# Retention pairs with both heads' scores in one matmul, queries decayed in turned form, a folded Fourier branch and nine steps a pair

## The chip, the cores and the metric

The kernel runs on one core of a Trainium2 chip. The metric is the device time of one execution in microseconds (us); the median of three runs of the kernel before is 1471.9. Engines are named as in the profile: PE (TensorE matmuls), DVE (VectorE), ACT (ScalarE), POOL (GpSimd), SP (the engine that issues most DMAs).

## The reference

Two transformer blocks over 512 positions of width 1024 in float32. The first (forgetting attention, a short convolution, a mixture of 16 experts, a per-layer embedding) is not touched by the change. The second has a bidirectional chunked retention, a Fourier mix, a gated merge of the two and a convolutional feed-forward part. The two branches that change, cut:

```
def chunk_retention(q, k, v, a, s0):        # 8 heads, dk 64, dv 128, CHUNK = 128
    diff = pos[:, None] - pos[None, :]
    intra_decay = where(diff >= 0, exp(lg * max(diff, 0)), 0)
    scores = einsum('bhncd,bhnsd->bhncs', qc, kc) * intra_decay
    intra = einsum('bhncs,bhnse->bhnce', scores, vc)
    k_dec = kc * exp(lg * (CHUNK - 1 - pos))
    kv = einsum('bhnsd,bhnse->nbhde', k_dec, vc)
    s_final, s_prev = scan(s -> exp(lg * CHUNK) * s + kv_n, s0, kv)
    q_dec = qc * exp(lg * (pos + 1))
    inter = einsum('bhncd,nbhde->bhnce', q_dec, s_prev)
    return intra + inter, s_final

o = chunk_retention(forward) + flip(chunk_retention(flipped))
o = (o - mean) * rsqrt(var + EPS)           # over dv, then * silu(g), then @ w_ret_out

def fourier_mix(f, w_f):                    # 4 groups of 128
    z = fft2(f.reshape(b, 512, 4, 128), axes=(1, 3), norm='ortho').real
    return z @ w_f
```

## The kernel before, in words

Every float32 matmul is made of three products of high and low parts: `split` (L186) writes the high part with a copy on ACT and the low part with a subtraction on DVE, `mm3` (L202) issues the three matmuls. Weights come by DMA into one of three `raw` slots (`new_raw`), are split into `whi` and `wlo` (`wsplit`), and a `Feed` (L117) keeps three weight splits ahead of the matmuls that use them. Tiles of 1024 columns come from a pool of 5 (`T`), of 512 columns from a pool of 35 (`B`); the accumulators come from four `pmm`, two `psd` and two `ptr` banks. A scheduler sets the order of each engine's instructions from the order of the program and its own estimate of readiness, so what stands side by side in a queue need not stand side by side in the code.

The retention works on pairs of heads, g = 0 to 3. `ret_proj(g)` projects q, k, v and the gate of pair g; q and k land as rows of positions in `qkr`. `ret_core` (L1504) turns q and k of a pair on PE (`pt_qk`, 8 transposes a pair), splits them, and loads the pair's decay factors `dmt` from a table `dmat` in HBM that `decays` (L637) has made early on. `ret_head` (L1547) is one head as a sequence of steps: queries and keys are decayed as rows of positions (tq and tk, L1553), the decayed queries are turned on PE (`pt_qd`, L1560) and split; scores of the head are 12 matmuls with 64 rows contracted (`ps_sc`), multiplied by the decay factors (`sc`, L1570) and split; `ps_kv` is 12 matmuls; the state recurrences (st, L1585 and L1588) work on the lower 64 partitions forward and the upper 64 backward; `ps_o` is 16 matmuls (L1604 to L1607). Then come `on` and its statistics on DVE, the reciprocal root on POOL (rs_e, rs_r), `nmr` on DVE, the normalisation `on` on ACT (L1626), the transposes `pt_o` (L1630) and the product with the gate (sg, L1631). `ret_cores` (L1528) deals the steps of a pair's two heads out in eight steps; a head's last steps are left for the next pair (`late`).

`fourier` (L1638) projects f in four groups of feature rows (`project`, `ps_f`, split into fT), multiplies along dims by a 128x256 table of cosines and sines (`along_dims`, two groups at a time: 24 matmuls of 256 columns, then half, fold and a split), and along rows by a table of 512x512 that is split in two pieces of 1024 columns (`along_rows`, 24 matmuls a group), into zT.

The driver sets the order: pair 0's projection runs alone, pairs 1 to 3 are projected while the steps of the pair before run beside them (a step of the retention for three of the projection), and the Fourier branch runs beside the last pair with ratio R_FOUR. Behind both come ret_out (`ps_ro`), which needs the split outputs `oT` of all pairs, the Fourier output, the branch gates and the merge.

```
    run(proj[0])
    cores = ret_cores()
    for g in range(1, 4):
        interleave(proj[g], islice(cores, 8), 1 / 3)
    interleave(four, cores, R_FOUR)
```

Of the kernel before, what the change touches and what calls it, by code (L numbers as in the profile page):

```python
# [21 lines left out]
P = 128  # L22
S = 512
# [14 lines left out]
R_FOUR = 0.37  # L38
# [9 lines left out]
def constants():  # L48
# [25 lines left out]
    once = np.concatenate([causal, tri, dec, dft1], 1)  # L74
    n = np.arange(S // 2)
    k = np.concatenate([2 * n, 2 * n + 1])
    w512 = 2 * np.pi * (np.outer(n, k) % S) / S
    dft2 = np.concatenate([np.cos(w512), -np.sin(w512)], 0) / 256.0
# [16 lines left out]
def weave(main, side, ratio, drain=True, acc=0.0):  # L95

    for _ in main:
        acc += ratio
        while side is not None and acc >= 1.0:
            acc -= 1.0  # L100
            next(side, 0)
        yield 1
    if side is not None and drain:
        yield from side
# [35 lines left out]
def fused_blocks(ctx, tc, a, out, probe=None, upto=99):  # L140
# [494 lines left out]
    dmat = drm.tile([P, D], F32, name="dmat")  # L635

    def decays():  # L637
# [21 lines left out]
        sp.dma_start(dmat, dm[0])  # L659
# [844 lines left out]
    def ret_core(g):  # L1504
# [5 lines left out]


        qkT = []
        for i in range(2):
# [3 lines left out]
            h, l = B("qk2_hi", F32R), B("qk2_lo", F32R)  # L1517
            if i == 0:
                act.activation(h, pt, AF.Copy, scale=0.125)
                dve.scalar_tensor_tensor(l, pt, 0.125, h.bitcast(F32), op0=ALU.mult, op1=ALU.subtract)  # L1520
            else:
                split(pt, h, l)
            qkT.append((h, l))
        dmt = B("dmt", w=256)
        sp.dma_start(dmt, dmat[:, 2 * c:2 * c + 256])
        return [ret_head(2 * g + hh, hh, rv, qkT, v, sg, dmt[:, hh * P:(hh + 1) * P]) for hh in range(2)]

    def ret_cores():  # L1528
# [3 lines left out]
        for g in range(4):  # L1532
            one_, two = ret_core(g)
# [13 lines left out]
    def ret_head(hd, hh, rv, qkT, v, sg, dmh):  # L1547

        tq, tk = B("tq"), B("tk")
        for tt, i in ((tq, 0), (tk, 1)):  # L1550
            tv = v3(tt, NT)
            for b in range(2):
                dve.tensor_scalar(tv[:, :, 64 * b:64 * b + 64], rv(i, hh), dec[:, 4 * b + i, hd:hd + 1], None,  # L1553
                                  op0=ALU.mult)
# [6 lines left out]
        qd = B("qd_hi", F32R), B("qd_lo", F32R)  # L1561
        split(pt, *qd)
        yield 1
        r = slice(64 * hh, 64 * hh + 64)
        ps = psd("ps_sc")
        for n in range(NT):
            cc = slice(n * P, n * P + P)
            mm3(ps[:, cc], [u[r, cc] for u in qkT[1]], [u[r, cc] for u in qkT[0]], True, True)
        sc = B("sc")
        dve.tensor_tensor(v3(sc, NT), v3(ps, NT), bc(dmh[:, None, :], [P, NT, P]), op=ALU.mult)  # L1570
        pT = B("sc_hi", F32R), B("sc_lo", F32R)
        split(sc, *pT)
# [25 lines left out]
        ps = [psd("ps_o") for _ in range(2)]  # L1598
        for n in range(NT):
# [3 lines left out]
            vn = v[n].rearrange("p (s h c) -> p h s c", s=2, h=2)[:, hh]  # L1603
            pe.matmul(hl, qd[0][:, cc], sn, start=True, stop=False)  # L1604
            pe.matmul(v3(hl, 2), pT[0][:, cc], vn, start=False, stop=False)
            pe.matmul(h, qd[1][:, cc], sn[:, :P], start=False, stop=False)
            pe.matmul(h, pT[1][:, cc], vn[:, 0], start=False, stop=True)  # L1607
# [30 lines left out]
    def fourier():  # L1638
# [3 lines left out]
        def load(i):  # L1642
            if i == 0:
                raw.append(new_raw())
                sp.dma_start(v3(raw[0], 4), a["k_dft2"].rearrange("(k p) c -> p k c", p=P))
            return wsplit(raw[0][:, i * 1024:(i + 1) * 1024], 1024)

        dft_nos = feed.plan([lambda i=i: load(i) for i in range(2)])

        def steps():  # L1650
            fT, aT, w = [], {}, []

            def project():
                f = len(fT)
                ps = yield from feat_step(nos[f // 2], h4, "ps_f2")
                h, l = B("fT_hi", F32R), B("fT_lo", F32R)
                split(ps, h, l)
                fT.append((h, l))

            def along_dims(gp):  # L1660

                for t in range(2):
                    ps = [pmm("ps_d1") for _ in range(2)]
                    for u in range(2):
                        for i in range(2):
                            x = [y[:, (t + 2 * u) * P:(t + 2 * u + 1) * P] for y in fT[2 * gp + i]]
                            mm3(ps[u][:, i * 256:i * 256 + 256], x, dft1, True, True)
# [194 lines left out]
```

## Time and profile before

| | |
|---|---|
| median of 3 runs | 1471.9 us (1471.68 to 1473.94) |
| the profiled execution | 1473.61 us |
| its span | 1471.5 us |
| mean granted PE clock | 0.994 |
| busy: PE, DVE, ACT, POOL | 1426.3, 989.4, 737.8, 115.5 us |

A span is the time from the first to the last instruction of the core. In the profile's rows a matmul's own duration overlaps that of the next one, so that the price of one in a row of many is the distance of two starts. The retention with the Fourier branch takes from about 700 to 888 us of the span: pairs begin (`pt_qk`) at 700.64, 745.46, 790.67 and 835.73, and ret_out begins at 888.52.

### The profile page before, as it was taken

The page shows a single profiled execution, that of the slowest core. Times are in us where ns is not written, and L with a number is a line of the kernel's source. Part 1 is how long each engine was busy: PE and PEld are TensorE (multiplying, and loading weights), DVE is VectorE, ACT ScalarE, POOL GpSimd, SP SyncE. Part 2 cuts the span into 40 slices and gives each one's busy share as a digit, 9 for nine tenths or more (in the row PEclk, how much of TensorE's full clock was granted, in tenths as well). Part 3 has the DMA queues.
Part 4 walks back from the last instruction along what each step waited for, and adds up shares of the span by engine and source line. Part 5 has one row for each costly group of instructions (what it writes and reads, how often), then busy time and mean ns, then how long its engine had stood idle before and what let it go on. Part 6 is the DMA issues. An engine that isn't in the chain of part 4 may idle for free.

```text
span 1471.5 us, 18307 instructions
## 1 busy us (share of the span) xinstructions
PE 1426.3 (97%) x6885; PEld 1156.6 (79%) x6885; DVE 989.4 (67%) x1590; ACT 737.8 (50%) x1201; POOL 115.5 (8%) x136
## 2 busy tenths in 40 slices
PE   6999999999999999799999999999999999999997
PEld 5777788887877676677888888888778888888886
DVE  6677764796899996655776777466665653465644
ACT  5765653434479887665444454334264442244422
POOL 1410000000031311200000000000000000000001
PEclk9999999999999999999999999999999999999999
DMA  6231234556679998323222115656623323343311
GB/s 227 71 123 59 81 121 156 174 202 257 195 253 375 394 389 309 131 67 105 89 63 90 62 58 170 202 175 212 201 57 93 108 79 97 97 115 86 104 54 57
DMA packets 150886, 219.15 MB, mean 149 GB/s; under 512 B 9728, under 2 KB 101388, under 8 KB 150796
## 3 DMA queue, kind: packets, MB, share of 16 engines
q1 hardware_dynamic: 145548, 201.05, 41.2%
q0 software_dynamic: 3456, 10.62, 2.2%
q10 hardware_dynamic: 1792, 6.29, 1.1%
q8 instruction: 55, 0.90, 0.2%
q14 instruction: 35, 0.29, 0.1%
HBM read 206.76 MB, written 11.17 MB: 148 GB/s over the span
## 4 chain that ended last, share of the span: by engine, by line
PE 53%; ACT 3%; DVE 2%; POOL 1%; issue 1%; POOLq 0%; ACTq 0%
PE ps_tok L206 6%; PE ps_tok L205 6%; PE ps_tok L204 6%; PE ps_up L204 6%; PE ps_up L205 6%; PE ps_up L206 6%; PE ps_gt L205 2%; PE ps_gt L206 2%; PE ps_gt L204 2%; PE ps_g L204 1%; PE ps_g L206 1%; PE ps_g L205 1%; PE ps_ro L204 1%; PE ps_ro L206 1%; PE ps_ro L205 1%
## 5 line engine op out<-in xcount | busy, mean ns | idle before, releaser
L188 DVE TENSOR_TENSOR wlo<-raw,whi 128x1024 fp32r<-128x1024 f32 x248 | 300.2, 1215 | 248.3 <-ACT whi L187 241.1
L187 ACT CAST whi<-raw 128x1024 fp32r<-128x1024 f32 x248 | 258.2, 1044 | 297.0 <-PE ps_tok L206 116.9
L204 PE MATMUL ps_up<-nt_hi,whi 128*128 128x512 f32 (+2 forms) x368 | 141.4, 385 | 2.8 <-ACT nt_hi L187 2.8
L205 PE MATMUL ps_up<-nt_lo,whi 128*128 128x512 f32 (+2 forms) x368 | 141.4, 384 | 0.0
L206 PE MATMUL ps_up<-nt_hi,wlo 128*128 128x512 f32 (+2 forms) x368 | 141.2, 384 | 0.0
L204 PE MATMUL ps_tok<-whi,nt_hi 128*128 128x512 f32 x288 | 115.2, 402 | 2.2 <-ACT nt_hi L187 2.1
L206 PE MATMUL ps_tok<-whi,nt_lo 128*128 128x512 f32 x288 | 113.1, 395 | 0.7 <-DVE nt_lo L188 0.7
L205 PE MATMUL ps_tok<-wlo,nt_hi 128*128 128x512 f32 x288 | 113.2, 395 | 0.0
L205 PE MATMUL ps_gt<-nt_lo,whi 128*128 128x512 f32 x256 | 99.6, 389 | 0.0
L204 PE MATMUL ps_gt<-nt_hi,whi 128*128 128x512 f32 x256 | 99.6, 389 | 0.0
L206 PE MATMUL ps_gt<-nt_hi,wlo 128*128 128x512 f32 x256 | 99.6, 389 | 0.0
L719 DVE SCALAR_TENSOR_TENSOR mod_acc<-raw,silu_c,mod_acc 128x1024 f32<-128x1024 f32 x56 | 70.7, 1279 | 20.2 <-DMA raw<-in_w_mod_dram 19.8
L204 PEld LDWEIGHTS ps_up<-nt_hi,whi 128*128 128x128 f32 x368 | 69.7, 190 | 16.0 <-ACT nt_hi L187 3.0
L205 PEld LDWEIGHTS ps_up<-nt_lo,whi 128*128 128x128 f32 x368 | 69.7, 189 | 13.3 <-DVE nt_lo L188 0.2
L206 PEld LDWEIGHTS ps_up<-nt_hi,wlo 128*128 128x128 f32 x368 | 69.7, 189 | 13.2
L188 DVE TENSOR_TENSOR wlo<-raw_a,whi 128x1024 fp32r<-128x1024 f32 x56 | 68.1, 1241 | 1.5 <-ACT whi L187 1.5
L204 PE MATMUL ps_tok<-whi,hid_hi 128*128 128x512 f32 x176 | 68.5, 389 | 0.0
L205 PE MATMUL ps_tok<-wlo,hid_hi 128*128 128x512 f32 x176 | 68.5, 389 | 0.0
L206 PE MATMUL ps_tok<-whi,hid_lo 128*128 128x512 f32 x176 | 68.3, 389 | 0.0
L204 PEld LDWEIGHTS ps_tok<-whi,nt_hi 128*128 128x128 f32 x288 | 54.7, 190 | 14.7 <-ACT nt_hi L187 3.6
L206 PEld LDWEIGHTS ps_tok<-whi,nt_lo 128*128 128x128 f32 x288 | 54.7, 190 | 13.0 <-DVE nt_lo L188 1.9
L187 ACT CAST whi<-raw_a 128x1024 fp32r<-128x1024 f32 x56 | 57.8, 1052 | 11.6 <-PE ps_tok L206 7.0
(461 smaller groups left out, 3291.8 us busy)
## 6 DMA issues: line engine op xcount, KB each, us to landing
raw<-in_w_in_dram SPq DMA_DIRECT2D x31, 1024.0 KB
raw<-in_w_up_dram SPq DMA_DIRECT2D x55, 512.0 KB
raw<-in_w_mod_dram SPq DMA_DIRECT2D x24, 1024.0 KB
raw<-in_w_down_dram SPq DMA_DIRECT2D x15, 1024.0 KB
raw_a<-in_w_gate_dram SPq DMA_DIRECT2D x19, 512.0 KB
raw_a<-in_w_up_dram SPq DMA_DIRECT2D x19, 512.0 KB
raw_a<-in_w_down_dram SPq DMA_DIRECT2D x9, 1024.0 KB
raw<-in_w_branch_gate_dram SPq DMA_DIRECT2D x8, 1024.0 KB
```

Source lines behind the costliest of these rows:

```text
L187: act.copy(hi, src)
L188: return (eng or dve).tensor_tensor(lo, src, hi.bitcast(F32), op=ALU.subtract)
L204: pe.matmul(ps, x[0], y[0], start=first, stop=False)
L205: pe.matmul(ps, x[0], y[1], start=False, stop=False)
L206: pe.matmul(ps, x[1], y[0], start=False, stop=last)
L719: dve.scalar_tensor_tensor(ac, rv[:, j, :], col, ac, op0=ALU.mult, op1=ALU.add)
```

## The change

- `decays`: beside the table for the scores a second one holds, for each head and both directions, the factors of the decayed queries in turned form (16 Exps of 64x128 on ACT, one more DMA of 512 KB); two small scalings on DVE go.
- `ret_core` is now a sequence of steps. The turned queries of both heads are split into tiles that hold the two heads in blocks of a diagonal, with zeros beside them (four memsets of 64x4x128 a pair on POOL), so that one matmul over 128 rows and 256 columns gives the scores of both heads: 12 matmuls a pair instead of 24. The decayed queries come from the turned ones in PSUM times the new factors (four instructions of 64x512 a pair on DVE); the transposes `pt_qd` go. `dmt` is 256 KB a pair, of 128 before, and is asked for ahead of `pt_qk`.
- `fourier` folds f along the feature axis before the matmuls along dims, so that each group needs 12 matmuls of 128 columns and 3 of one output row; the table along rows is folded too, 128x1024, one DMA of 512 KB and one split, and takes 12 matmuls a group. Its split stands at the start of the branch's code. Dims and rows of the groups alternate with the projections.
- A pair has nine steps, steps can weigh less than one, and R_FOUR is 0.5.

```diff
 def weave(main, side, ratio, drain=True, acc=0.0):
-    for _ in main:
-        acc += ratio
+    for step in main:
+        acc += ratio * step
...
+        for h in range(8):
+            r = slice(64 * (h % 2), 64 * (h % 2) + 64)
+            for b in range(2):
+                o = h // 2 * 256 + b * P
+                act.activation(dq[r, o:o + P], C("iota")[r, :], AF.Exp, ...)
+        sp.dma_start(dmat[:, 1], dq)
...
-        dmt = B("dmt", w=256)
-        sp.dma_start(dmt, dmat[:, 2 * c:2 * c + 256])
+        dmt = B("dmt")
+        sp.dma_start(v3(dmt, 2), dmat[:, :, 2 * c:2 * c + 256])
...
+        for u in q4:
+            for hh in range(2):
+                pool.memset(u[64 * hh:64 * hh + 64, :, 1 - hh, :].bitcast(F32), 0.0)
+        for hh, r in enumerate(rows):
+            act.activation(q4[0][r, :, hh, :], pts[0][r], AF.Copy, scale=0.125)
+            dve.scalar_tensor_tensor(q4[1][r, :, hh, :], pts[0][r], 0.125, q4[0][r, :, hh, :].bitcast(F32),
+                                     op0=ALU.mult, op1=ALU.subtract)
+        split(pts[1], *[v3(u, NT) for u in kT])
+        yield [ret_head(2 * g + hh, hh, rv, v, sg, qds, pT) for hh in range(2)]
+        for r in rows:
+            tq = B("tq")
+            for b, o in enumerate(rows):
+                dve.scalar_tensor_tensor(v3(tq, NT)[o], pts[0][r], 0.125,
+                                         bc(dmt[r, None, 256 + b * P:384 + b * P], [64, NT, P]),
+                                         op0=ALU.mult, op1=ALU.mult)
+            qd = B("qd_hi", F32R), B("qd_lo", F32R)
+            split(tq, *qd)
+            qds.append(qd)
+        yield
+        for j in range(2):
+            ps = psd("ps_sc")
+            for n in (2 * j, 2 * j + 1):
+                mm3(ps[:, n % 2 * 256:n % 2 * 256 + 256], [u[:, n * P:n * P + P] for u in kT],
+                    [u[:, n * 256:n * 256 + 256] for u in qb], True, True)
+            sc = B("sc")
+            dve.tensor_tensor(v3(sc, 2), v3(ps, 2), bc(dmt[:, None, :256], [P, 2, 256]), op=ALU.mult)
+            pT.append((B("sc_hi", F32R), B("sc_lo", F32R)))
+            split(sc, *pT[j])
...
-            for step in ((one_, late), (one_, two, late), (one_,), (two,), (one_,), (two, one_), (one_,), (two,)):
+            for step in ((core, late), (core, one_), (two,), (one_,), (two,), (one_,), (two, one_), (one_,)):
...
-        pt = ptr("pt_qd")
-        for t in range(NT):
-            pe.transpose(pt[:, t * P:(t + 1) * P], tq[:, t * P:(t + 1) * P], ident)
...
                 ps = yield from feat_step(nos[f // 2], h4, "ps_f2")
+                x, uv, y = B("f_rows"), B("f_half"), B("f_fold")
+                act.copy(x, ps)
+                for i, op in enumerate((ALU.add, ALU.subtract)):
+                    dve.tensor_tensor(uv[:, 256 * i:256 * i + 256], x[:, :256], x[:, 256:], op=op)
+                for i, op in enumerate((ALU.add, ALU.subtract)):
+                    dve.tensor_tensor(y4[:, 2 * i:2 * i + 2, 1:], uv2[:, :, 1:P], uv2[:, :, 255:P:-1], op=op)
+                act.copy(y4[:, 0::3, 0], uv4[:, 0::2, 0])
+                act.copy(y4[:, 2:0:-1, 0], uv4[:, 1::2, 0])
+                split(y, h, l)
...
-            for part in (project(), project(), project(), along_dims(0), project(), along_dims(1),
-                         along_rows(0), along_rows(1), along_rows(2), along_rows(3)):
+            for part in (project(), project(), along_dims(0), project(), along_dims(1), along_rows(0), project(),
+                         along_dims(2), along_rows(1), along_dims(3), along_rows(2), along_rows(3)):
...
-        interleave(proj[g], islice(cores, 8), 1 / 3)
+        interleave(proj[g], islice(cores, 9), 9 / 24)
```

The first place is ACT, at the end of pair 2 and the start of the last pair. Before (o_half and on are the outputs of one head, qk_hi the splits of the turned q and k):

```order
L1626 ACTIVATE on<-on,nmr,rs_r 128x128 x4
L187 CAST sc_hi<-sc 128x512
L1582 COPY st<-s_6233 64x128
L1583 COPY st<-s_6233 64x128
L187 CAST st_hl<-st 128x2x128 x2
L187 CAST whi<-raw 128x1024
L1446 ACTIVATE sg_8259<-ps_g 128x512
L187 CAST whi<-raw 128x1024
L1612 COPY o_half<-ps_o 128x256 x2
L1446 ACTIVATE sg_8342<-ps_g 128x512
L1626 ACTIVATE on<-on,nmr,rs_r 128x128 x4
L1519 ACTIVATE qk_hi<-pt_qk_8369 128x512
```

Now (qb_hi and k_hi are the splits of the turned q and k):

```order
L1657 ACTIVATE on<-on,nmr,rs_r 128x128 x4
L1643 COPY o_half<-ps_o 128x256 x2
L1657 ACTIVATE on<-on,nmr,rs_r 128x128 x2
L1459 ACTIVATE sg_8312<-ps_g 128x512
L1657 ACTIVATE on<-on,nmr,rs_r 128x128 x2
L191 CAST whi<-raw 128x1024
L1543 ACTIVATE qb_hi<-pt_qk_8345 64x4x128
L191 CAST k_hi<-pt_qk_8350 128x512
L1543 ACTIVATE qb_hi<-pt_qk_8345 64x4x128
```

Before, the second head's o_half stood behind other work and well after the first head's on; now it stands directly behind the first head's on, the on of both heads stand close together, and the splits of the last pair behind both.

On DVE, what stands around the last pair's splits now (qb_lo are the splits of the two heads' queries, sg the product with the gate, wlo a weight's low part):

```order
L1653 SCALAR_TENSOR_TENSOR nmr<-mv,rs_r 128x4
L1662 TENSOR_TENSOR sg_7754<-sg_7754,pt_o 128x512
L192 TENSOR_TENSOR wlo<-raw,whi 128x1024
L1544 SCALAR_TENSOR_TENSOR qb_lo<-pt_qk_8345,qb_hi 64x4x128
L192 TENSOR_TENSOR k_lo<-pt_qk_8350,k_hi 128x512
L1544 SCALAR_TENSOR_TENSOR qb_lo<-pt_qk_8345,qb_hi 64x4x128
L1552 SCALAR_TENSOR_TENSOR tq<-pt_qk_8345,dmt 64x512 x2
L1662 TENSOR_TENSOR sg_7841<-sg_7841,pt_o 128x512
L192 TENSOR_TENSOR wlo<-raw,whi 128x1024
L192 TENSOR_TENSOR qd_lo<-tq,qd_hi 128x512
L1552 SCALAR_TENSOR_TENSOR tq<-pt_qk_8345,dmt 64x512 x2
```

Before, two qk_lo stood directly behind nmr, and qd_lo behind transposes on PE; now sg and a wlo stand ahead of the splits, tq reads dmt, and qd_lo stands behind tq.

The second place is PE, where the first matmuls along dims (ps_d_8498, of fT of group 0) now stand among those of the third Fourier projection (ps_f_8524):

```order
L210 MATMUL ps_f_8419<-nt_hi,wlo 128x512
L208 MATMUL ps_d_8498<-dft_hi,fT_hi 128x128
L209 MATMUL ps_d_8498<-dft_lo,fT_hi 128x128
L208 MATMUL ps_f_8524<-nt_hi,whi 128x512
L209 MATMUL ps_f_8524<-nt_lo,whi 128x512
L210 MATMUL ps_f_8524<-nt_hi,wlo 128x512
L208 MATMUL ps_f_8524<-nt_hi,whi 128x512
L210 MATMUL ps_d_8498<-dft_hi,fT_lo 128x128
```

Before, the first matmuls along dims stood behind three whole projections.

The third place is SP's queue around the last pair's dmt, now:

```order
L1525 DMA dmt<-dmat 128x2x256
L1677 DMA raw<-in_k_dft_dram 128x1024
L280 DMA raw<-in_w_in_dram 128x8x256
L280 DMA raw<-in_w_ret_out_dram 128x8x256 x2
L1525 DMA dmt<-dmat 128x2x256
L723 DMA raw<-in_w_mod_dram 128x2x1024
```

The last dmt stands behind two ret_out weight loads, as before, and takes twice the bytes; the Fourier table, which stood behind the last projections' weights, is now loaded ahead of the last of them.

## Rows read from the trace of the kernel before

**Rows 1.** The page, part 1: busy time, share of the span and instructions of each engine.
```profile
PE 1426.3 (97%) x6885; PEld 1156.6 (79%) x6885; DVE 989.4 (67%) x1590; ACT 737.8 (50%) x1201; POOL 115.5 (8%) x136
```

**Rows 2.** Windows, pairs 0 to 2: busy us (instructions) per engine, PE clock, DMA share, GB/s.
```profile
700.00:745.00 45.00, 45.00 (x246) 38.24 (x245) 32.38 (x88) 18.60 (x36) 2.13 (x4) 1.00 0.28 87
745.00:790.00 45.00, 45.00 (x248) 38.34 (x248) 32.90 (x90) 19.94 (x40) 2.44 (x5) 1.00 0.23 75
790.00:830.00 40.00, 40.00 (x220) 33.91 (x219) 29.32 (x78) 17.91 (x37) 2.23 (x3) 1.00 0.21 67
```

**Rows 3.** Timeline of PE: start us, us, engine, line, operation, out<-in, shape, count.
```profile
831.56 0.45 PE L204 MATMUL ps_f<-nt_hi,whi 128*128 128x512 f32 x1
...
835.73 1.03 PE L1516 MATMUL pt_qk<-misc,qkr 128*128 128x128 f32 x8
...
845.76 0.32 PE L204 MATMUL ps_sc<-qk_hi 64*128 64x128 f32 x1
...
847.24 0.33 PE L204 MATMUL ps_kv<-v,kd_hi 128*128 128x128 f32 x1
...
853.27 0.28 PE L204 MATMUL ps_d<-dft_hi,fT_hi 128*128 128x256 f32 x1
...
854.69 0.28 PE L1604 MATMUL ps_o<-st_hl,qd_hi 128*128 128x256 f32 x1
...
888.52 0.40 PE L204 MATMUL ps_ro<-oT_hi,whi 128*128 128x512 f32 x1
```

**Rows 4.** The chain of waits, 825 to 895: start us, us, what.
```profile
825.38 0.44 PE pt_o L1630 x4
...
835.04 1.05 POOL rs_r L381
...
890.51 0.52 ACT oT_hi L187
```

**Rows 5.** Windows, the last pair's stretch on DVE, columns as in rows 2.
```profile
838.47:884.57 46.10, 42.96 (x284) 37.99 (x282) 37.88 (x86) 23.95 (x49) 3.15 (x4) 1.00 0.14 47
```

**Rows 6.** Timeline of DVE, last pair; in brackets idle before and releaser.
```profile
838.47 0.69 DVE L1520 SCALAR_TENSOR_TENSOR qk_lo<-pt_qk,qk_hi 128x512 fp32r<-128x512 f32 x1 [2.20 <-ACT qk_hi L1519]
...
839.68 0.61 DVE L1553 TENSOR_SCALAR tq<-qkr,dec 128x256 f32<-128x256 f32 x2
840.20 0.61 DVE L1553 TENSOR_SCALAR tk<-qkr,dec 128x256 f32<-128x256 f32 x2
840.73 1.21 DVE L188 TENSOR_TENSOR wlo<-raw,whi 128x1024 fp32r<-128x1024 f32 x1
...
850.25 0.69 DVE L188 TENSOR_TENSOR sc_lo<-sc,sc_hi 128x512 fp32r<-128x512 f32 x1 [0.74 <-ACT sc_hi L187]
850.86 0.33 DVE L1585 SCALAR_TENSOR_TENSOR st<-st,g,ps_kv 64x128 f32<-64x128 f32 x1
851.22 0.35 DVE L1588 SCALAR_TENSOR_TENSOR st<-st,g,ps_kv 64x128 f32<-64x128 f32 x1
...
853.62 0.76 DVE L188 TENSOR_TENSOR st_hl<-st,st_hl 128x256 fp32r<-128x256 f32 x2 [0.53 <-ACT st_hl L187]
```

**Rows 7.** The instructions of L853: count, ns min/median/max, first and last start.
```profile
L853 DVE SCALAR_TENSOR_TENSOR q_hl<-pt_qk,gq,q_hl x8: 743/749/756, 81.8 to 163.4; 64x512 fp32r<-64x512 f32 x8
```

**Rows 8.** Timeline of ACT at the last pair's start.
```profile
836.31 1.65 ACT L1626 ACTIVATE on<-on,nmr,rs_r 128x128 f32<-128x128 f32 x4 [3.67 <-DVE nmr L1622]
```

**Rows 9.** Timeline of ACT, 58 to 80.
```profile
62.45 0.99 ACT L655 ACTIVATE dm_f<-once,eneg 128x128 f32<-128x128 f32 x3
...
78.81 1.05 ACT L187 CAST whi<-raw 128x1024 fp32r<-128x1024 f32 x1 [4.39 <-PE ps_tok L206]
```

**Rows 10.** Groups of POOL by form: count, busy us, mean ns, idle before.
```profile
L779 POOL TENSOR_TENSOR kdc<-kc,dec 128x256 f32<-128x256 f32 x8 | 11.0, 1398 | 0.1
```

**Rows 11.** Timeline of SP's queue, 815 to 840.
```profile
821.21 11.23 SPq L276 DMA_DIRECT2D raw<-in_w_ret_out_dram  x2
```

**Rows 12.** DMA issues, 80 to 180: count, KB each, median us to landing.
```profile
q_hc<-crows POOLq DMA_DIRECT2D x6, 8.0 KB, 2.4
```

More of the change, by code (lines that the diff above doesn't have):

```diff
@@ L1526, in ret_core @@
-        return [ret_head(2 * g + hh, hh, rv, qkT, v, sg, dmt[:, hh * P:(hh + 1) * P]) for hh in range(2)]
+            pts.append(v3(pt, NT))
+        qb = [T("qb_" + u, F32R) for u in ("hi", "lo")]
+        q4 = [u.rearrange("p (n h c) -> p n h c", h=2, c=P) for u in qb]
+        for u in q4:
+            for hh in range(2):
+                pool.memset(u[64 * hh:64 * hh + 64, :, 1 - hh, :].bitcast(F32), 0.0)
+        kT = [B("k2_" + u, F32R) for u in ("hi", "lo")]
+        rows = [slice(64 * hh, 64 * hh + 64) for hh in range(2)]
@@ L1528, in ret_cores @@
+        yield
     def ret_cores():
@@ L1532, in ret_cores @@
         for g in range(4):
-            one_, two = ret_core(g)
-            for step in ((one_, late), (one_, two, late), (one_,), (two,), (one_,), (two, one_), (one_,), (two,)):
+            core = ret_core(g)
+            next(late, 0)
+            one_, two = next(core)
+            yield 1
+            for step in ((core, late), (core, one_), (two,), (one_,), (two,), (one_,), (two, one_), (one_,)):
                 for h in step:
@@ L1545, in ret_cores, with ret_head @@
             yield 1
[L1547 to L1554, printed above, removed]
+    def ret_head(hd, hh, rv, v, sg, qds, pT):
+        tk = B("tk")
+        tv = v3(tk, NT)
+        for b in range(2):
+            dve.tensor_scalar(tv[:, :, 64 * b:64 * b + 64], rv(1, hh), dec[:, 4 * b + 1, hd:hd + 1], None, op0=ALU.mult)
         kd = B("kd_hi", F32R), B("kd_lo", F32R)
@@ L1557, in ret_head @@
         yield 1
-        pt = ptr("pt_qd")
-        for t in range(NT):
-            pe.transpose(pt[:, t * P:(t + 1) * P], tq[:, t * P:(t + 1) * P], ident)
[L1561 to L1572, printed above, removed]
         ps = psd("ps_kv")
@@ L1603, in ret_head @@
             vn = v[n].rearrange("p (s h c) -> p h s c", s=2, h=2)[:, hh]
+            pn = [u[:, (n % 2 * 2 + hh) * P:(n % 2 * 2 + hh + 1) * P] for u in pT[n // 2]]
             pe.matmul(hl, qd[0][:, cc], sn, start=True, stop=False)
[L1605 removed]
+            pe.matmul(v3(hl, 2), pn[0], vn, start=False, stop=False)
             pe.matmul(h, qd[1][:, cc], sn[:, :P], start=False, stop=False)
[L1607 removed]
+            pe.matmul(h, pn[1], vn[:, 0], start=False, stop=True)
         on = B("on")
@@ L1640, in fourier @@
         raw = []
[L1642 to L1648, printed above, removed]
-        def steps():
-            fT, aT, w = [], {}, []
+        def steps():
+            fT, aT = [], []
+            w = [T("dft2_hi", F32R), T("dft2_lo", F32R)]
+            raw = new_raw()[:, :1024]
+            sp.dma_start(raw, a["k_dft2"])
+            split(raw, *w)
             def project():
```

84 lines of the change are left out of this document (37 added, 47 removed).

## The prediction

> **What bounds the kernel now.** I read the page's first part, then a table by stage, then the chain of waits, and then the timelines of PE, DVE, ACT and SP around the places that the chain names. The profiled execution took 1473.6 us, 1471.5 of it the span; the median shown is 1471.9, so a sum made against the profile is lowered by 1.7 to stand on the median. A change under 0.2% (2.9 us) can't be told from none here.
>
> PE is busy 97% of the span [rows 1]. In the stretches in which pairs 0 to 2 run beside the next pair's projection it is busy every microsecond, 45.00 of 45, 45.00 of 45 and 40.00 of 40, while DVE works 32.4, 32.9 and 29.3 [rows 2]. A matmul taken out there is time taken out, as long as DVE and ACT keep up. The last pair, which runs beside the Fourier branch, is another matter. From the first Fourier projection (831.56) to the first ret_out matmul (888.52) are 56.96 us [rows 3]; the chain leaves PE there, runs through POOL's rsqrt and the splits on DVE and ACT, and is on ACT's oT_hi just ahead of ps_ro [rows 4]. From DVE's first split of q (838.47) to its first split behind the last a_lo (884.57) are 46.1 us: DVE is busy 37.9 of them and idle 8.2, PE is busy 43.0 [rows 5]. Both engines are near their limit in that stretch.
>
> **The change on PE.** The spacing of starts is the price of one matmul. Eight turned queries a pair go; four transposes cost 0.44 on the chain [rows 4], so 0.9. The scores of one head, 12 matmuls, took from 845.76 to 847.24, of two heads 2.96; they become 12 matmuls of 256 columns, which took 1.42 along dims (853.27 to 854.69, 0.118 each) [rows 3]: 1.5 less. That is 2.4 us a pair, 9.6 in all. Along rows 96 matmuls of 256 columns become 48: 5.7 less. Along dims 48 of them (5.7) become 48 of 128 columns and 12 with one output row; at no more than 0.118 each that is 7.1, 1.4 more, and if the one-row ones cost nothing it is no more; I take 1.0 more. PE's whole saving is 9.6 + 5.7 - 1.0 = **14.3 us**; 1459.3 on the profile, 1457.6 on the median, is the floor.
>
> **DVE and ACT.** A pair's queries are now decayed in turned form, in four instructions of 64x512 in place of four of 128x256 (two in 0.52, 839.68 to 840.20) [rows 6]. The nearest row to the new ones is L853, the same operation on 64 partitions, 0.749 us [rows 7]. Full-width neighbours overlap: sc_lo lasts 0.69, and its successor starts 0.61 after it. The st instructions, which alternate between the lower and the upper 64 partitions, last 0.33 and start 0.36 apart: none overlaps [rows 6]. So I take 0.75 for each of the six that alternate in a pair (four tq, two qb_lo): tq costs 2.0 more, and two qb_lo and a k_lo in place of two qk_lo 0.9 more. The Trainium skill (VectorE: DVE Perf Modes, "Two Vector instructions with no wait between them") has a rule that speaks against these six: an instruction whose input or output starts in another group of 32 partitions than the last one's is held until all earlier ones are done. The st rows agree with it. If it didn't hold for them, they would cost 0.61 like full-width ones, the last pair would be 0.84 shorter, and the sum 1467.7 instead of 1468.5.
>
> In the Fourier branch 8 folds and 4 of 8 splits of a go (0.6 each): 7.2. In their place come 8 f_half and 8 f_fold of 256 columns; at 0.34, between tq's 0.26 and st_hl's 0.38 (two in 0.76 [rows 6]), that is 5.4: 1.8 less. The order now puts two z_lo (0.6 each) ahead of the last a_lo: 1.2 more. DVE's work in the stretch becomes 37.9 + 2.0 + 0.9 - 1.8 + 1.2 = **40.2 us**: the folding takes work from PE, not from DVE. ACT is busy 24 of the 46 [rows 5]; its new copies count only as links of a chain.
>
> **Pairs 0 to 2.** DVE gets 2.9 us more a pair and has 11 to 13 idle in each [rows 2], so the first two keep the whole 2.4. Pair 2 gets the split of the Fourier constant (1.2, as wlo [rows 6]) and the lag that its predecessors pass on; of its 2.4 I count 0.6. Together 5.4; the ends are 2.4 (one pair gains) and 7.2 (all three).
>
> **The last pair**, from the first Fourier projection on, is start + work + idle + what follows.
> Start: pt_qk came 4.2 after that projection began [rows 3], behind 18 matmuls; now it stands behind 12, at 2.7. DVE's first split came 2.7 behind pt_qk [rows 3, 6], so it starts at 5.5 at best. But on ACT the second head's o_half of pair 2 now stands behind the first head's on, and the first qb_hi behind both heads' on, so that two rounds through POOL follow each other; in one of them on waited 3.7 for nmr and held ACT from 836.31 to 837.96 [rows 8]. Twice the lag, 5.4, makes it 8.1. I take the middle, 6.8 (now 6.9).
> Work: 40.2.
> Idle: 8.2 if chains cover each other as now. The order sets six more dependent pairs of instructions side by side on DVE, each a round trip through ACT of 0.7 (sc_lo waited 0.74 [rows 6]): a qd_lo, a second sc_lo, a kd_lo and three fT_lo. All paid, 12.4. I take 10.3.
> After the last a_lo stand 12 matmuls along rows, 1.4, with 0.2 of hand-over: 1.6.
> 6.8 + 40.2 + 10.3 + 1.6 = 58.9, against 56.96 now: **2.0 longer**, although PE has some 7 us less to do there. PE will wait at the first ps_d for fT_hi, at ps_kv for kd, and for the last two heads' ps_o and pt_o.
>
> **Edits at nothing.** Of the 16 Exps for the queries' factors eight stand before dm_f at about 61 us: 0.3 each (three dm_f in 0.99), 2.5 us, ahead of 4.4 us in which ACT waits for PE at 78.81 [rows 9]; without that cover, 2.5. The other eight fall into the attention, another 2.5 if PE waited for ACT there. The table's second 512 KB is written long before it is read. The 16 memsets run on POOL, busy 8% [rows 1]; no row shows their size, the nearest (kdc, 256 columns, 1.40 [rows 10]) makes 2.8 each an upper end, and nothing the lower. On SP the last dmt waits behind two ret_out loads, whose issue lasted until 832.44 for want of a raw slot [rows 11]. tq reads it some 9 us after the stretch begins, where the scores read it later; a load of 8 KB lands in 2.4 us [rows 12]. If the slot is freed as now it costs nothing, if it is freed by the wlo that stands just ahead of qb_lo, up to 2.5.
>
> **Sum:** 1473.6 - 5.4 + 2.0 = 1470.2, on the median **1468.5 us**; with the ends of pairs and idle its own range is 1465 to 1472.5.
>
> **Rivals.**
> *PE's saving is kept* (0.28). For it: the order splits the first ps_d group among f2's matmuls, as if fT were there in time, and DVE has 6 us more idle room than work added. With the early start and today's idle the stretch is 5.5 + 40.2 + 8.2 + 1.6 = 55.5, 1.5 shorter, and all pairs give 7.2: 1473.6 - 8.7 - 1.7 = 1463.2. Against it: the six round trips. It holds if they are hidden.
> *The last pair grows by more than the pairs gave: slower* (0.21). The place is DVE's queue between on of pair 2 and tq of pair 3: a late start (8.1), dmt 2.5 late with all behind tq queued, and all round trips paid: 8.1 + 2.5 + 40.2 + 12.4 + 1.6 = 64.8, 7.8 longer. If pairs give 4.8, 1473.6 + 3.0 - 1.7 = 1474.9; if one pair gains, 1477.3. It decides once the stretch is over 62.3 with one pair's gain, 65.3 with mine. For it: the wlo ahead of qb_lo and the raw slot in front of dmt.
> *The change moves nothing* (0.06): ret_out starts when its weights and oT are split, and the chain did lie on oT_hi there [rows 4]. If that sets the end, or the Exps lose their cover, it stays at 1471.9.
>
> **How the numbers follow.** The forecast holds 0.45, the rivals 0.28, 0.21 and 0.06. Faster by over 0.2%, below 1469.0, are nearly all of the first rival (0.27) and a little over half of the forecast (0.25): 0.52. Within 0.2% are 0.18 of the forecast, the last rival's 0.06, 0.02 of the slower one and 0.01 of the first: 0.27. Slower are 0.19 of its rival and 0.02 of the forecast: 0.21. The range goes down to 1460.5, so that only cases near the floor are out, and up to 1477.0, near the slower rival with one pair.
>
> **What would show it.** Pair starts (pt_qk) 42 to 43 us apart in place of 45; the distance from the first ps_f to ps_ro near 59, with PE idle 10 to 15 of it and DVE busy 40; tq at 0.75 without overlap; 12 ps_sc in 1.4. It is wrong if pairs stay at 45, or if the distance falls below 55 or rises over 62.

## The result and the profile after

The changed kernel takes 1485.49 us (median) against 1471.88: a ratio of 1.0093 [1.0077, 1.0109]. One of its four executions took 2855.94 us and is left out here; with it the median is 1486.45, from which the expectations below start. The forecast was 1468.5, its range ended at 1477.0; the change makes the kernel slower by 13.6 us. The profiled executions stand 11.7 apart (1485.27 and 1473.61; that of after is the lowest of its runs, that of before among the higher ones). The accounting below is between these two.

| | before | after | difference | predicted |
|---|---|---|---|---|
| span | 1471.5 | 1483.1 | +11.6 | -3.4 |
| first pt_qk begins | 700.5 | 701.9 | +1.4 | 0 |
| from there to the first ps_f | 131.1 | 136.1 | +5.0 | -5.4 |
| from there to the first ps_ro | 57.0 | 62.8 | +5.8 | +2.0 |
| the rest | 583.0 | 582.4 | -0.6 | 0 |

PE is busy 4.2 us less than in [rows 1], in 116 matmuls fewer, where 14.3 were forecast; part of the rest is that, as shown below, some matmuls now run at a lower clock and take longer. DVE is busy 8.4 more. The page, part 1, of after:

```profile
PE 1422.1 (96%) x6769; PEld 1153.4 (78%) x6769; DVE 997.8 (67%) x1596; ACT 747.4 (50%) x1224; POOL 119.3 (8%) x152
```

The windows of the kernel before over pairs 0 to 2 (columns as in rows 2):

```profile
700.48:831.56 131.08, 131.08 (x723) 111.73 (x722) 95.34 (x257) 57.62 (x114) 6.80 (x10) 1.00 0.24 75
```

Those of after: pairs 0 to 2, the whole last stretch, DVE's part of it (which answers to rows 5), and three slices of 4 us in pair 0:

```profile
701.86:837.94 136.08, 127.88 (x663) 109.15 (x662) 106.09 (x270) 60.36 (x118) 12.73 (x21) 0.96 0.25 79
837.94:900.71 62.77, 54.28 (x295) 47.80 (x294) 42.43 (x96) 29.20 (x63) 3.57 (x5) 0.84 0.16 51
843.49:898.47 54.98, 46.49 (x249) 40.88 (x248) 39.96 (x93) 24.04 (x53) 2.54 (x4) 0.82 0.18 58
...
728.00:732.00 4.00, 1.80 (x13) 1.50 (x11) 3.72 (x14) 1.23 (x4) 0.00 (x0) 0.97 0.94 290
732.00:736.00 4.00, 3.44 (x12) 3.18 (x13) 3.19 (x14) 1.35 (x4) 0.00 (x0) 0.50 0.13 42
736.00:740.00 4.00, 4.00 (x13) 3.12 (x13) 1.73 (x5) 3.08 (x6) 1.28 (x2) 0.68 0.00 0
```

Before, PE was busy in every microsecond of the pairs at clock 1.00 (its last stretch, too, ran at 1.00). Now it stands still for 8.2 us of them and runs for a while at half its clock. The timeline of PE in pair 0 shows both, and further on the marks that answer to rows 3 (in brackets the idle time before and its releaser):

```profile
729.53 0.27 PE L1638 MATMUL ps_o<-v,sc_lo 128*128 128x128 f32 x1
732.56 0.55 PE L1635 MATMUL ps_o<-st_hl,qd_hi 128*128 128x256 f32 x1 [2.76 <-DVE st L1617]
...
734.30 0.73 PE L208 MATMUL ps_g<-nt_hi,whi 128*128 128x512 f32 x1
734.83 0.63 PE L209 MATMUL ps_g<-nt_lo,whi 128*128 128x512 f32 x1
...
837.94 0.48 PE L208 MATMUL ps_f<-nt_hi,whi 128*128 128x512 f32 x1
...
840.78 1.03 PE L1532 MATMUL pt_qk<-misc,qkr 128*128 128x128 f32 x8
...
900.71 0.90 PE L208 MATMUL ps_ro<-oT_hi,whi 128*128 128x512 f32 x3
```

The second half of a head's ps_o waits 2.76 us for a state update. The timeline of DVE shows whose:

```profile
724.73 0.35 DVE L1617 SCALAR_TENSOR_TENSOR st<-st,g,ps_kv 64x128 f32<-64x128 f32 x1
...
730.18 0.33 DVE L1614 SCALAR_TENSOR_TENSOR st<-st,g,ps_kv 64x128 f32<-64x128 f32 x1
...
732.06 0.35 DVE L1617 SCALAR_TENSOR_TENSOR st<-st,g,ps_kv 64x128 f32<-64x128 f32 x1
```

The first head's last st ended at 725.08 and its split was long done; the wait is for the *second* head's last st, which ends at 732.41. These matmuls don't read it. `psd` has two banks. The nine steps issue ps_kv of both heads ahead of ps_o of the first; the second bank that ps_o needs is still held by the second head's ps_kv, until DVE has read it. DVE came to it at 730.18, behind a weight's wlo and the rope (rotation by position), qkr and v of the next projection. The waits of PE from 700 to 901 (total us, times, longest):

```profile
PE ps_o L1635 <- DVE st L1617: 9.2, 4, 2.8
PE ps_d L208 <- ACT fT_hi L191: 5.1, 2, 2.8
PE ps_o L1635 <- DVE st_hl L192: 2.0, 1, 2.0
```

So the bank is waited for once in every pair, the folded projection twice in the last. The waits of DVE in its part of the last stretch, 843.6 to 898.5:

```profile
DVE wlo L192 <- ACT whi L191: 2.6, 2, 2.1
DVE sg L1662 <- PE pt_o L1661: 2.5, 1, 2.5
DVE fT_lo L192 <- ACT fT_hi L191: 2.2, 3, 0.7
DVE nmr L1653 <- POOL rs_r L385: 2.1, 2, 1.5
DVE sc_lo L192 <- ACT sc_hi L191: 1.4, 2, 0.7
DVE kd_lo L192 <- ACT kd_hi L191: 1.4, 2, 0.7
```

A third wait of wlo, 2.54 us, ends at 842.35, ahead of this part. The longest wait of wlo in it, on DVE, and what stands ahead of its whi on ACT:

```profile
889.38 1.23 DVE L192 TENSOR_TENSOR wlo<-raw,whi 128x1024 fp32r<-128x1024 f32 x1 [2.06 <-ACT whi L191]
...
886.76 1.65 ACT L1657 ACTIVATE on<-on,nmr,rs_r 128x128 f32<-128x128 f32 x4 [1.45 <-DVE nmr L1653]
888.32 1.03 ACT L191 CAST whi<-raw 128x1024 fp32r<-128x1024 f32 x1
```

At its end the stretch waits for PE as well. The chain of waits lies on DVE, ACT and POOL up to 873.86, on PE from there to 881.05, and on PE again from 892.82 to ps_ro. The timeline of PE, first where it runs 15 matmuls along dims at full clock, then the same 15 of the last group, four transposes and the first 12 matmuls along rows; below it the window of these, with its clock:

```profile
886.91 0.22 PE L208 MATMUL ps_d<-dft_hi,fT_hi 128*128 128x128 f32 x1
...
888.38 0.33 PE L208 MATMUL ps_d<-dft_hi,a_hi 128*128 128x256 f32 x1
...
892.82 0.48 PE L208 MATMUL ps_d<-dft_hi,fT_hi 128*128 128x128 f32 x1 [2.80 <-ACT fT_hi L191]
...
896.06 1.07 PE L1661 MATMUL pt_o<-misc,on 128*128 128x128 f32 x4
896.79 0.56 PE L208 MATMUL ps_d<-dft_hi,a_hi 128*128 128x256 f32 x1
...
899.28 0.28 PE L208 MATMUL ps_d<-dft_hi,a_hi 128*128 128x256 f32 x1
```

```profile
892.82:898.86 6.04, 6.00 (x29) 5.82 (x29) 3.16 (x5) 1.55 (x3) 0.00 (x0) 0.50 0.37 144
```

From 892.82 to 899.28 are 6.5 us. At full clock the 15 along dims took 1.5 (886.91 to 888.38), four transposes 0.44 [rows 4], 12 along rows 1.4 (899.28 to 900.71), together 3.4. By this reckoning the lowered clock behind the last wait costs about 3 us at the end of the chain.

Near 62 us the timeline of ACT answers to rows 9:

```profile
63.66 2.51 ACT L662 ACTIVATE dm_q<-misc,eneg 64x128 f32<-64x128 f32 x5
```

### The profile page after: what moved, and what is told of

Same layout as the page of the kernel before. It is cut to its first block, busy times and chain, and to the rows that moved or that the text cites. A ratio compares the mean times of both kernels' runs of the same rounds, so it can differ in the third digit from the quotient of the medians.

```text
span 1483.1 us, 18105 instructions
## 1 busy us (share of the span) xinstructions
PE 1422.1 (96%) x6769; PEld 1153.4 (78%) x6769; DVE 997.8 (67%) x1596; ACT 747.4 (50%) x1224; POOL 119.3 (8%) x152
## 4 chain that ended last, share of the span: by engine, by line
PE 49%; DVE 5%; ACT 3%; POOL 2%; issue 1%; POOLq 0%; ACTq 0%; DVEq 0%
PE ps_tok L210 6%; PE ps_tok L209 6%; PE ps_tok L208 6%; PE ps_up L208 6%; PE ps_up L210 5%; PE ps_up L209 5%; PE ps_gt L210 2%; PE ps_gt L208 2%; PE ps_gt L209 2%; PE ps_ro L209 1%; PE ps_ro L208 1%; PE ps_ro L210 1%; PE pt_n L459 1%; POOL rs_r L385 1%; DVE wlo L192 1%
```

## The experiments

The kernel before is run beside each; ratios are to it, and what an edit is worth is read from its distance to that run, held against the 13.6 of the whole change. "Pairs" is the distance from the first pt_qk to the first ps_f (131.1 before, 136.1 after), "stretch" that from the first ps_f to the first ps_ro (57.0 and 62.8). Where not said otherwise, the edit is made to the changed kernel. The theories in the expectations: A, the pairs lose by psd's bank; C, the last stretch grows by the folded Fourier chain; D, by the retention's own part; F, chains through ACT and DVE set it, whichever wait of PE is taken away; G, PE's waits and the clock behind them are the price.

**e1, ps_kv in another bank.**

```diff
-        ps = psd("ps_kv")
+        ps = ptr("ps_kv")
```

> The changed kernel with one word changed: ps_kv takes its accumulator from the two ptr banks instead of the two psd banks. The order on PE and DVE stays the same up to two rows. Theory A (a bank): the second half of the first head's ps_o waits because its bank is still held by ps_kv of the second head, until DVE's last st has read it (idle 2.76, 2.80 and 2.64 us in pairs 0 to 2, 1.03 in the last). Then these four waits go, and so does the lower PE clock right behind two of them (0.50 from 732 to 738): 9.2 and some 3.3 us, to 1474 us (1472 to 1477). Theory B (DVE's queue is late, whatever the bank): the waits stay at the same matmuls, now behind st_hl, and the time stays within 3 us of 1486.5.

1482.04, ratio 1.0061 [1.0044, 1.0078]. Pairs 130.0, at clock 1.00; pair 0 takes 42.2, as forecast, pairs 1 and 2 take 45.5 and 45.1. The windows of the pairs, then PE's waits in them:

```profile
702.58:832.59 130.01, 126.48 (x664) 105.46 (x662) 103.22 (x259) 58.83 (x117) 12.37 (x20) 1.00 0.26 83
```

```profile
PE ps_o L1635 <- DVE on L1644: 2.0, 2, 1.4
PE pt_qk L1532 <- DVE sg L1662: 0.6, 2, 0.3
```

A has the place right: the waits for st are gone and 6.1 us of the pairs with them. But the time misses the ranges of both A and B. New waits for on and for sg stand in pairs 1 and 2, on banks that DVE frees late, and the last stretch grows by 2.8, to 65.6: PE waits 1.6 there at pt_qk and 1.5 at pt_o, which share the two ptr banks with ps_kv now. With both, the edit is worth 4.4 of the 13.6 (9.3 are left).

**e2, ps_o of the first head ahead of the second's ps_kv.**

```diff
-            for step in ((core, late), (core, one_), (two,), (one_,), (two,), (one_,), (two, one_), (one_,)):
+            for step in ((core, late), (core, one_), (one_,), (two,), (one_,), (two, one_), (one_,), (two,)):
```

> The changed kernel with the nine steps of a pair in another order: the first head's ps_o comes before the second head's ps_kv, as it did before the change; banks as in the change. Theory A (a bank): the waits in the middle of the first ps_o go, about 1474 to 1478 us. Theory B (DVE's queue is late): ps_o of the first head stands nearer to its own state recurrence, waits for st_hl 2 to 4 us a pair, and the time is 1484 to 1490.

1488.15, 1.0105 [1.0088, 1.0122]; pairs 135.4, stretch 66.7. The waits for st are gone, others stand in their place; PE's, 700 to 836:

```profile
PE ps_kv L208 <- ACT kd_hi L191: 3.0, 3, 1.4
PE ps_kv L208 <- DVE on L1644: 2.3, 2, 1.4
PE pt_o L1661 <- ACT on L1657: 2.3, 1, 2.3
```

The nine-step order had bought room between the scores and ps_kv, and paid with the bank.

**e3, the 16 Exps later.** They become `decay_q()`, called behind the forgetting attention's output.

```diff
-        dq = T("dm_q")
...
+    decay_q()
```

> The changed kernel with only the 16 Exps moved behind the attention's output, where ACT is less than half busy. If their early place costs what the trace shows (PE waits 1.0 us for ACT's qn at 71 us, and the first ps_s 2.2 us instead of 0.7), both waits return to what they were and the time falls by 1 to 2.5 us, to 1484 to 1485.5. If ACT's idle time after 74 us takes them in, as my sum had it, the time stays within 0.7 of 1486.5.

1484.2, 1.0088 [1.0071, 1.0105], against 1.0093 [1.0077, 1.0109] for the whole change: the times can't tell the two apart. The traces say some 1 us. The early waits of PE (0.99 for qn, 2.2 for q_hl) are those of before again (0.7 for q_hl), and the first pt_qk comes at 700.9 for 701.9. Over all profiled executions of the new retention it comes at 700.8 to 704.6 with the Exps in their early place (eight, mean 702.8) and at 700.3 to 702.6 with them moved (five, mean 701.6).

**e4, the new retention with the old Fourier branch** (table, fourier and R_FOUR 0.37 of before).

> The changed retention with the Fourier branch, its table and R_FOUR of the kernel before. Both theories leave the waits of pairs 0 to 2 where they are. Theory C (the folded Fourier's chain f_rows, f_half, f_fold, fT sets the last stretch): the stretch from the first Fourier projection to ps_ro falls from 62.8 to 57 to 59 although PE has 4.7 us more to do, time 1481 to 1483. Theory D (the retention's own queue on DVE sets it): the stretch is 62 to 67, time 1486 to 1491.

1487.47, 1.0092 [1.0075, 1.0108]; pairs 134.7, stretch 63.0: D. The new retention alone makes the stretch as long as the whole change does, at a clock of 0.95 there and of 1.00 from 880 to its end.

**e5, the kernel before with the new Fourier branch** (folded tables, fourier, R_FOUR 0.5).

> The kernel before with the folded Fourier branch alone (its table, the steps' weights, R_FOUR 0.5); retention as before. Pairs 0 to 2 begin as before (45 us apart). Theory C: the folded chain lengthens the last stretch, 57 to 61 us where it was 56.96, time 1472 to 1476. Theory D: the folding's saving on PE comes through, stretch 52.5 to 56, time 1467.5 to 1471.

1474.4, 1.0007 [0.9998, 1.0017]; pairs 131.1, stretch 60.8: C as well. The fold alone adds 3.8 to the stretch, though it takes matmuls out. So 6.0 and 3.8 make 5.8 together, not 9.8: the two don't add. The clock falls behind a wait of 2.16 at pt_qd and again behind one of 2.6 for fT_hi at the end, where the window up to ps_ro is:

```profile
884.00:891.97 7.97, 7.68 (x40) 7.54 (x40) 4.34 (x7) 3.06 (x6) 0.00 (x0) 0.57 0.25 103
```

**e6 and e7, other work as cover.** The Fourier output's projection runs beside the last pair, ahead of ret_out; e7 is the same on the kernel before, with 0.25. The stretch is then read from the first ps_f to the first ps_gt (the branch gates): 123.9 before, 129.3 after.

```diff
-    interleave(four, cores, R_FOUR)
+    interleave(four, cores, 0.3, False)
+    interleave(f_out, cores, 0.8)
```

> The changed kernel with the order behind the Fourier branch changed: the Fourier output's 96 matmuls, which need no retention, now stand ahead of ret_out, and the last pair's steps run beside the Fourier branch (0.3 a step) and beside these (0.8 a step). Theory E (the last pair's chains on DVE and ACT lack other PE work beside them, and each PE stall of about 2 us or more is followed by some us of PE at clock 0.50): the stalls of the last stretch shrink below 2 us, PE stays at 1.00 there, 1474 to 1479 us; the waits in pairs 0 to 2 stay. Theory F (the folded Fourier's own chain makes the stalls, ahead of the output's matmuls): the two waits for fT_hi (2.3 and 2.8 us) and the lowered clock behind them stay, only those at ps_o and pt_o go, 1481 to 1485.

1481.15, 1.0068 [1.0046, 1.0091]; 120.7 to ps_gt, 8.6 less; from there to the end, where that work is now missing as company, the time grows by 2.4 (518.3 against 515.9). One wait of 3.8 for fT_hi remains; the time is at the edge of F's range.

> The kernel before with the same new place for the Fourier output's matmuls (last pair's steps at 0.25 a step beside the Fourier branch, 0.8 beside them). Its last stretch holds only some 3 us of PE waits and no lowered clock, so theory E leaves it little to gain: 1468.5 to 1472.5. Theory F says the same. If it gains over 4 us, the cover is worth that to any kernel, and the change's own part has to be read against it.

1481.62, 1.0061 [1.0044, 1.0078], and 129.5 to ps_gt: a miss. On the kernel before the same cover costs 5.7 up to ps_gt and 3.3 behind it (519.4 against 516.1): its stretch had no waits of that size to fill. It is no gain by itself.

**e8, e1 with e3 and e6.**

> The changed kernel with three edits: ps_kv in the ptr banks, the Fourier output ahead of ret_out as above, and the 16 Exps of the queries' factors moved behind the attention's output. Theory E with A: pairs 0 to 2 take 128 to 131 us, the last stretch keeps its clock, 1464 to 1470, faster than both kernels. Theory F: 1476 to 1480.

1475.7, 1.0021 [1.0012, 1.0031], another miss. The first ps_gt comes at 952.9 where after has it at 967.2, 14.3 earlier, but the part behind it gives back 5.3 (521.2 against 515.9). The longest wait in PE's timeline there is 3.31 us, for mod_hi at 1045.52.

**e10, e8 with more side work there** (`R_G2` 0.18 for 0.15).

> The kernel with all three edits, and the side work behind it (the second modulation's rows) at 0.18 a step instead of 0.15, because its main work got shorter by the 96 matmuls that were moved. There a new wait stood at 1042 to 1045.5 (PE for mod_hi, 3.31 us) with a lowered clock behind it. Without it 1475.7 becomes 1470 to 1473. If the time stays at 1475, that wait was not on the path.

1476.27, 1.0021 [1.0011, 1.0032]; 2.40 of that wait remain, nothing is gained. The Fourier wait of 3.80 for fT_hi, at 875.53, is still there too.

**e9, e10 with the Fourier parts in another order** (and 0.2 and 0.95 for 0.3 and 0.8).

```diff
-            for part in (project(), project(), along_dims(0), project(), along_dims(1), along_rows(0), project(),
+            for part in (project(), project(), along_dims(0), project(), project(), along_dims(1), along_rows(0),
```

> As the last, and the last pair's steps at 0.2 a step beside the Fourier branch and 0.95 beside its output, the four Fourier projections ahead of the second group along dims: DVE folds all four groups before the last pair's state recurrences. Theory E (a PE wait of some us in the last stretch costs itself and then PE at clock 0.50): the wait of 3.80 us for the last fT_hi and the lowered clock from 872 to 880 go, 1463 to 1469, faster than both kernels. Theory F (the folded chain is too long in any order): waits for fT_hi or a_hi of 2 us and more remain, 1470 to 1474.

1476.59, 1.0020 [1.0010, 1.0030]. The wait for fT_hi is gone, that for a_hi has taken its place, and longer:

```profile
868.59 0.58 PE L208 MATMUL ps_d<-dft_hi,a_hi 128*128 128x256 f32 x1 [4.54 <-ACT a_hi L191]
```

**e12, the same order of parts on e5.**

> The kernel before with the folded Fourier branch alone, and its four projections ahead of the second group along dims. With the branch alone the last stretch held two waits followed by a lowered clock: 2.16 us at pt_qd and, at the end, 2.60 us at the last group along dims for fT_hi. Theory G with E: the second goes, as the last projection is now 51 matmuls ahead of it, with some 3 us of lowered clock behind it: 1474.4 falls to 1468 to 1471, faster than the kernel before. Theory F (DVE's work in the stretch sets its end, in whatever order): the end moves by less than 2 us, 1472.5 to 1476.

1474.03, 1.0009 [1.0000, 1.0018]; stretch 60.4 for 60.8. Again the wait moves (1.78 for a_hi) and the time stays, in F's range. But the lowered clock moves with it, 0.54 from 880 to ps_ro, so that this run doesn't test what the clock costs there.

**e11, useless matmuls in the bank wait.** Nothing reads their product.

```diff
+            if n == 2 and hh == 0 and hd < 6:
+                fill = ptr("fill")
+                for _ in range(12):
+                    pe.matmul(fill, qd[0][:, :P], pT[0][0], start=True, stop=True)
```

> The changed kernel with PE work added: 12 matmuls of 512 columns that nothing reads (2.7 us at full clock) into a ptr bank, between the two halves of the first head's ps_o in pairs 0 to 2, where PE waited 2.76, 2.80 and 2.64 us. Theory G (the wait is paid twice, once as idle and once as the lower PE clock behind it): PE now works through the wait, its clock stays at 1.00 in pairs 0 to 2, and though the kernel does 8.2 us more of PE work the time falls by 3 to 6 us, to 1480.5 to 1483.5. Theory H (the clock falls for another reason, or costs nothing beside the wait): the clock falls as before or the time does not, 1486 to 1489.

1482.93, 1.0068 [1.0052, 1.0084]: 10.7 over the kernel before instead of 13.6, so 2.9 *less* than after, with work added. No execution of it (1481.8 to 1484.3) is as long as the shortest of after. Pairs 132.5, stretch 63.8. The same three slices as shown of after:

```profile
728.00:732.00 4.00, 4.00 (x23) 3.43 (x23) 3.85 (x14) 1.23 (x4) 0.00 (x0) 1.00 0.54 154
732.00:736.00 4.00, 4.00 (x22) 3.24 (x21) 3.18 (x10) 1.36 (x4) 0.00 (x0) 1.00 0.55 178
736.00:740.00 4.00, 4.00 (x23) 3.40 (x22) 2.12 (x12) 1.67 (x3) 1.28 (x2) 1.00 0.00 0
```

The bank is as late as ever, but the clock stays at 1.00 and in the 12 us 68 matmuls run, 12 of them useless, in place of 38. In these pairs a wait was paid twice: G. The pairs are 3.6 shorter than in after; in e3, e4, e13 and e14, whose edits leave them alone, they took 134.6 to 136.5, so that the clock's part is 2 to 4 us. The gain stands where the clock had fallen: 2.8 in pair 0 and 0.9 in pair 2. In pair 1 (45.5 and 45.6) there is none, and there after's clock had stayed at 1.00 behind a wait of 2.80. The same wait of pair 1 in e13 (2.79) did lower it. A window behind it in after, then in e13:

```profile
780.00:784.00 4.00, 3.13 (x18) 2.77 (x19) 3.34 (x13) 2.13 (x5) 0.00 (x0) 1.00 0.21 65
...
780.00:784.00 4.00, 4.00 (x15) 3.42 (x16) 3.07 (x13) 1.60 (x5) 0.32 (x2) 0.57 0.04 13
```

**e13, the same in the last stretch** (10, 8, 5 and 12 useless matmuls at its waits).

> The changed kernel with 35 matmuls of 512 columns that nothing reads (7.9 us at full clock) in the last stretch, where PE waited: 10 ahead of the first group along dims (2.29 us), 8 and 5 at the first head's ps_o (1.95 and 1.03), 12 ahead of the last group along dims (2.80). Theory G (the lowered clock behind each wait is a price of its own): PE stays at 1.00 in the last stretch, which falls from 62.8 to 57 to 60 us, 1481 to 1484. Theory F (DVE's and ACT's chains set the stretch; the slower PE only fills time in which it would wait): the clock stays at 1.00 but the stretch stays within 1.5 us of 62.8 and the waits move, 1485 to 1488.

1486.45, 1.0087 [1.0072, 1.0102]; stretch 65.5, 2.7 longer, a miss of both ranges. Two windows of it, and a wait that remains:

```profile
852.00:892.00 40.00, 35.88 (x213) 29.49 (x212) 27.29 (x72) 17.91 (x44) 2.53 (x4) 1.00 0.08 27
896.00:904.01 8.01, 7.76 (x41) 7.77 (x42) 3.82 (x7) 2.19 (x4) 0.00 (x0) 0.57 0.21 88
```

```profile
895.52 0.33 PE L208 MATMUL ps_d<-dft_hi,fT_hi 128*128 128x128 f32 x1 [2.39 <-ACT fT_hi L191]
```

The run doesn't settle the clock's part. Up to 892 the clock stays at 1.00 and the stretch gains nothing by it. But the order on ACT changed as well: the second head's o_half, ahead of the first head's on in after (881.08), stands behind it here (884.93), and DVE's on waits for it. And behind the wait that remains the clock is at 0.57 up to ps_ro, as in after: the 3 us at the end of the chain are still there.

**e15, e1, e3 and e13 in one.**

> The changed kernel with ps_kv in the ptr banks, the Exps behind the attention's output, and the fillers of the last stretch. If the three costs are separate they add up: 1486.5 less 4.4 (bank), 2.3 (Exps) and 3 to 5 (clock, theory G) makes 1475 to 1477, not faster than the kernel before. By theory F 1479 to 1481.

1482.7, 1.0064 [1.0050, 1.0078]; pairs 129.8, but the stretch 67.1, where e1 alone had 65.6: beyond both theories. The fillers didn't keep the clock up here (0.92 over the stretch); why the stretch is longer still wasn't followed up.

**e14, no fold:** the projection is split straight from PSUM.

```diff
-                x, uv, y = B("f_rows"), B("f_half"), B("f_fold")
...
-                split(y, h, l)
+                split(ps, h, l)
```

> The changed kernel without the fold: the Fourier projections are split as they are (f_rows, the two f_half, the two f_fold and the two small copies are left out, four times), so the Fourier branch computes something else; PE's work is the same. DVE has 6 us less to do in the last stretch, and each projection's chain to its first matmul is 2.9 us shorter. Theory F: the stretch falls by 5 us or more, to 54 to 58, time 1478 to 1482. Theory G: the two waits for fT_hi shrink under 1.5 us and the clock behind them stays up, which gives 4 to 7 us as well; so the waits are what tells: if the stretch falls by 5 us while waits with a lowered clock remain, it is DVE's work.

1478.64, 1.0036 [1.0023, 1.0050]; the windows of the stretch:

```profile
839.86:893.87 54.01, 47.46 (x296) 41.37 (x294) 36.57 (x80) 25.52 (x51) 3.47 (x5) 0.97 0.18 59
```

54.0 for 62.8. PE does the same matmuls, DVE 5.9 less, ACT 3.7 less, and the links f_rows, f_half and f_fold go from the chain between a projection and its ps_d. DVE's work, the chain and most of the lowered clock go together here (0.97 over the stretch for 0.84; PE is busy 6.8 us less in as many matmuls); which of the three weighs most isn't told apart.

No version beat the kernel before; the nearest are e12 and e5, which can't be told from it. Two things were not tried: a run of after that takes away the lowered clock at the end of the last stretch alone, and R_FOUR alone, which sets where the last pair's steps stand among the Fourier matmuls.

## Why the prediction was wrong

**The pairs.** Both of the prediction's signs of being wrong came: pairs begin 47.8, 45.5 and 45.6 apart, and the stretch is over 62. The step that failed is "so the first two keep the whole 2.4", with its sum "Together 5.4". It asked whether DVE had idle time in the pair, not when DVE would reach the reads that free PE's accumulators. The new order put one such read, the second head's last st, ahead of ps_o. The saving is real where nothing waits (pair 0 in e1: 42.2). But without the bank wait the three pairs gain 1.1 together, not 5.4, with DVE busy for 103.2 of 130.0 where it was 95.3 of 131.1: an idle share of a fifth didn't put its reads in time.

**The clock.** No term of the sum let PE's granted clock fall, since rows 2 show 1.00 throughout. e11 puts 2 to 4 us of the pairs' loss on it, and about 3 more stand at the end of the chain in the last stretch, by the trace of after alone.

**The last stretch.** The working was start 6.8, work 40.2, idle 10.3, behind it 1.6. Measured in after: 5.6 (837.94 to 843.49), 40.0, 15.0, and 2.2 to ps_ro. The work was right to 0.2, in part by luck: tq came cheaper than taken (0.69 for 0.75), f_half and f_fold dearer (0.38 for 0.34). The start was better than feared. The failed term is the idle time, "I take 10.3". The six listed round trips were all paid, some 4.2, which makes its upper end of 12.4; what no list held is that wlo waits 2.6 for ACT, where it waited 0.5 before, and sg 2.5 for pt_o. In the longer of wlo's two waits, 2.06, its whi stands on ACT behind a head's on, which itself waits for nmr; in the other, 0.51, behind the fold's two small copies. The working counted ACT's copies "only as links of a chain" and not as a queue in which whi stands behind others. The sg waits for a pt_o that stands on PE behind the last group along dims, which waited 2.80 for fT_hi and then ran at half clock; the same clock is in the 2.2 where 1.6 was taken. e4 and e5 show that either half of the change lengthens the stretch by itself, e14 that the stretch is 8.8 shorter without the fold's work and links. How much of the 5.8 is chains through DVE and ACT and how much the clock at their end stays open: e4 has 6.0 with the clock at 1.00 at its end, the trace of after puts about 3 on a lowered one there, and e13 doesn't decide.

**The edits at nothing.** "0.3 each" for the Exps was 0.49 each back to back, 3.9 for the first eight, and the cover named, ACT's 4.4 us behind them, came too late: PE waited 0.99 and 1.5 more for what stood behind them on ACT. In the traces it is some 1 us up to the first pt_qk (e3), where nothing was taken. The late dmt cost nothing (asked for at 827.66). That tq doesn't overlap came out as taken: two in 1.38 at 845.55, 0.69 each. This agrees with the rule of the Trainium skill (VectorE: DVE Perf Modes, "Two Vector instructions with no wait between them") that the prediction names. 12 ps_sc in 1.4 were right too.

**The rivals.** The slower one had the sign and the engine (DVE's queue), not the mechanism: it looked for a late dmt in the last pair, and a large part of the loss is a bank in pairs 0 to 2. Of the 11.6 between the profiled spans, 1.4 lie ahead of the first pt_qk, 5.0 in the pairs, where the bank with the clock behind it is 6.1 (e1, which loses 2.8 of it again behind them), and 5.8 in the last stretch, which no edit that keeps the computation took away. The medians stand 2.0 further apart than the two profiled executions; that much isn't placed.

## What to carry to other kernels

When a change takes matmuls out or deals their steps out anew, write down for each PSUM bank who reads it last, and how far down that reader stands in its engine's queue: the wait falls on a matmul that doesn't use the data. Work that is folded from PE into a chain of DVE and ACT must fit beside that chain's links, not only into its idle total. Useless matmuls in a PE wait can tell apart what the wait costs and what the clock behind it costs: in e11 time came back, and the order on the other engines was that of after. They decide nothing where they also change another engine's order or leave the last wait as it is (e13): look at both, and at the clock up to the end of the stretch, before reading the time.

## What was not expected of the hardware

- Behind a PE wait of 2.76 us the granted clock was 0.50 (its level of 1.2 GHz) from 732 to 736, and 0.68 in the next 4 us; ps_g starts stood 0.42 to 0.53 apart for 0.23. Behind the waits of 1.4 in e1 it stayed at 1.00, and so it did behind the 2.80 of pair 1 in after; behind the 2.79 of the same place in e13 it was 0.57. The length of a wait alone doesn't tell whether the clock falls, though theory E (e6) took it so.
- The 64x128 Exps took 0.49 to 0.50 each, without overlap (five in 2.51); dm_f, of twice the size, took 0.33 (three in 0.99). The 64x128 ones alternate between the halves of the partitions and take a bias from a tile as well as a scale; which of the two it is wasn't told apart.
- Adding 36 matmuls made the changed kernel 2.9 us faster (e11).
